# Moving x and u by 96 bytes inside their partitions in a transformer block kernel

## The chip, the cores and the metric

The kernel runs on one core of one Trainium2 chip. The metric is the time of one execution in microseconds (us) on the device; the kernel before was run three times. A profile is one further execution, recorded instruction by instruction. Engines are called as the profile calls them: PE is TensorE's matmul stream, PEld its weight loads, DVE is VectorE, ACT is ScalarE, POOL is GpSimd, SP is SyncE.

## The reference

One block over 256 tokens of width 1024, in float32: an RMS norm, one wide input projection, causal attention with 8 heads beside a gated depthwise convolution with a layer norm, an output projection with residual, a second RMS norm, a gated feed-forward network of width 2816 with residual, and a last RMS norm. Cut to what matters:

```python
u = rms_norm(h, mix_norm_g[l])
proj = u @ w_in[l]                                   # 1024 x 2560
q, k, v, glu_a, glu_g = jnp.split(proj, splits, axis=-1)
attn_out = moba_attention(heads(q), heads(k), heads(v), rel_bias)
conv_out = conformer_conv(glu_a, glu_g, conv_w[l], conv_b[l], conv_ln_g[l], conv_ln_b[l])
h = h + jnp.concatenate([attn_out, conv_out], axis=-1) @ w_out[l]
u = rms_norm(h, ffn_norm_g[l])
h = h + (jax.nn.silu(u @ w_gate[l]) * (u @ w_up[l])) @ w_down[l]
return rms_norm(h, final_norm_g)
```

With 256 tokens the attention has one block of keys, so only the causal part of it is left.

## The kernel before, in words

Every large product is made from float32 operands that are split in two: a rounded upper part and the remainder, so that a product takes three matmuls: upper by upper, upper by lower, lower by upper. For the weights, `high` makes the upper part `wh` (a copy on ACT, for two pieces on DVE) and `split` the lower part `wl` (a subtraction on DVE). For the activations, the upper part `uh` and the lower part `ul` lie in one tile, `u2`, of 8 row blocks by 2 parts by 256 tokens; `xs` holds x (later the hidden state) in 8 row blocks of 256 tokens. `xs` and `u2` come from the pool `const`, the first in memory, and the weights' parts `wh_...` and `wl_...` from the pool `wts` right behind it.

A matmul has two operands in SBUF: the stationary one, 128 columns that a weight load brings into the array ahead of it, and the moving one, which streams past. Each matmul here has a weight load of its own. Which operand is u differs from stage to stage, and so does the length of the stream:

- the input projection's convolution half (`a_mm`, outputs `pa` and `pg`) and its queries and keys (`qk_mm`, outputs `pqk`): weights stationary, u moving, 256 columns;
- the values (`v_mm`, output `pv`): u stationary, weights moving, 512 columns;
- the output projection (`o_part`, output `py`): weights stationary, moving the tiles `mh` and `ml` (the upper and lower part of the attention and convolution outputs), 256 columns;
- gate and up projection (`up_mm`, output `pf`): u stationary, weights moving, 512 columns; 48 matmuls for each of 11 groups of 256 hidden units;
- the down projection (`down`, output `pd`): stationary `fh` and `fl`, the two parts of the gated activations, weights moving, 512 columns, 24 matmuls for each group; its last quarters (output `pe`) have streams of 256 columns.

The order of the first part, up to the end of the output projection, is written out by hand in the string `PROGRAM`; after it, groups of `pf` and `pd` alternate, `down(g - 1)` behind `gate_up(g + 1)`. SP issues the loads of the weights in that order, two tensors ahead. PE, and every engine, keeps its instructions in program order.

Places in a partition, in bytes, of the built programs (the remainder by 128 in brackets). A tile's operands lie at its base plus multiples of 512 bytes, in the input, output, gate, up and down projections all.

| tile | before | after |
|---|---|---|
| `mhalf` (the exponent -0.5) | 42848 (96) | 16512 (0) |
| `xs` | 16512 (0) | 16608 (96) |
| `u2` | 24704 (0) | 24800 (96) |
| `pv` (vectors) | 41088 (0) | 41184 (96) |
| `ones`, `ident` | 41824, 42336 (96) | 41984, 42496 (0) |
| first `wh` buffer; all `wh`, `wl` and raw weights alike | 72800 (96) | 72928 (96) |
| first `fh` buffer; all `fh`, `fl` alike | 183392 (96) | 183520 (96) |
| `mh`, `ml` | 203520, 212736 (0) | 203648, 212864 (0) |

Of the kernel before, what the change touches and what calls it, by code (L numbers as in the profile page):

```python
# [10 lines left out]
F32 = mybir.dt.float32  # L11
F32R = mybir.dt.float32r
AF = mybir.ActivationFunctionType
ALU = mybir.AluOpType

P = 128
# [16 lines left out]
Q = 6  # L33
# [19 lines left out]
PV_G1, PV_G2, PV_CB, PV_LG, PV_LB, PV_T = 0, 8, 16, 20, 24, 28  # L53
PV_CW = PV_T + CC * ONV
PV_FOLD = PV_CW + 16 * Q
PV_N = PV_FOLD + 32
# [3 lines left out]
def block_kernel(ctx, tc, xT, w_in, w_out, w_gu, w_down, pvec, gfin, relb, hot, out):  # L60
    nc = tc.nc
    const = ctx.enter_context(tc.tile_pool(name="const", bufs=1))
# [8 lines left out]
    def mm(*args, **kw):  # L71
        return tc.keep_in_program_order(nc.tensor.matmul(*args, **kw))  # L72
# [12 lines left out]
    act, vec, pool, sync = (InOrder(e) for e in (nc.scalar, nc.vector, nc.gpsimd, nc.sync))  # L85

    def bank(i, name):
        return psum.tile([P, 512], F32, tag=f"b{i}", name=name)
# [76 lines left out]
        return mm(o, wl, uh, start=False, stop=stop, skip_group_check=True)  # L165


    xs = const.tile([P, KD, S], F32, name="xs")
    u2 = const.tile([P, KD, 2, S], F32R, name="u2")
    uh, ul = u2[:, :, 0], u2[:, :, 1]  # L170
    pv = const.tile([P, PV_N], F32, name="pv")
    ones = const.tile([P, P], F32, name="ones")
    ident = const.tile([P, P], F32, name="ident")
    mhalf = const.tile([P, 2], F32, name="mhalf")
    warm = const.tile([P, 1], F32, name="warm")
    accx = w1.tile([P, S], F32, name="accx")
    rbt = w1.tile([NB + 1, H], F32, name="rbt")
# [25 lines left out]
        pool.memset(t[:, TAPS - 1 + S : UW + TAPS - 1], 0.0)  # L203
        pool.memset(t[:, UW + TAPS - 1 + S :], 0.0)
    pool.memset(invc, 1.0 / (CC * P))
    pool.dma_start(pv[:, PV_T:], pvec[:, PV_T:])

    col = lambda lo, i: pv[:, lo + i : lo + i + 1]


    def conv_weights(half):
        fold, cw = pv[:, PV_FOLD:], pv[:, PV_CW + half * 8 * Q :]
        vec.tensor_tensor(
            wstk[half],
            bass.AP(tensor=fold.tensor, offset=fold.offset, ap=[fold.ap[0], [0, 8 * Q], [1, 32]]),
            bass.AP(tensor=cw.tensor, offset=cw.offset, ap=[cw.ap[0], [1, 8 * Q], [0, 32]]), op=ALU.mult)
# [3 lines left out]
    def rstd(acc, n, eps, name, b):  # L220
        ps = bank(b, f"ps_{name}")
        for t in range(2):
            mm(ps[:, t : t + 1], acc[:, t * P : (t + 1) * P], ones[:, 0:1], start=True, stop=True)
        ms = const.tile([P, 2], F32, name=f"ms_{name}")
        vec.tensor_scalar(ms, ps[:, 0:2], 1.0 / n, eps, op0=ALU.mult, op1=ALU.add)
        rc = const.tile([P, 2], F32, name=f"rc_{name}")
        pool.tensor_tensor(rc, ms, mhalf, op=ALU.pow)
        dg = const.tile([P, S], F32, name=f"dg_{name}", tag="dg")
        for t in range(2):
            vec.tensor_scalar(dg[:, t * P : (t + 1) * P], ident, rc[:, t : t + 1], None, op0=ALU.mult)  # L230
        return rc, dg
# [28 lines left out]
    cw = lambda c: csq[0][:, c]  # L260
# [74 lines left out]
    def scale_x():  # L335
        xn["c"], xn["d"] = rstd(accx, D, RMS_EPS, "x", 5)
# [147 lines left out]
    def norm(part):  # L484
        if part == 1:
            vec.tensor_add(s4[:, 0], s4[:, 0], s4[:, 1])
        elif part == 2:
            pm = bank(2, "pm")
            mm(pm[:, :S], invc, s4[:, 0], start=True, stop=True)
            for c in range(CC):  # L490
                vec.tensor_sub(cv(c), cv(c), pm[:, :S])
        elif part == 6:
            csq.append(w1.tile([P, CC, S], F32, name="csq", tag="wstk", bufs=2))
            for c in range(CC):
                act.activation(cw(c), cv(c), AF.Square)
        elif part == 3:
            vec.tensor_add(s4[:, 0], cw(0), cw(1))
            vec.tensor_add(s4[:, 1], cw(2), cw(3))
            vec.tensor_add(s4[:, 0], s4[:, 0], s4[:, 1])
        elif part == 7:  # L500
            _, ln["dg"] = rstd(s4[:, 0], CC * P, LN_EPS, "ln", 4)
        elif part == 4:
            ln["r"] = wide(ln["dg"], "ln", 5)
        else:
            for c in range(CC):
                vec.tensor_mul(cv(c), cv(c), ln["r"][:, :S])
                act.activation(cw(c), cv(c), AF.Silu, scale=col(PV_LG, c), bias=col(PV_LB, c))
                act.copy(mix[0][:, 4 + c], cw(c))
            for c in range(CC):
                vec.tensor_sub(mix[1][:, 4 + c], cw(c), mix[0][:, 4 + c].bitcast(F32))  # L510
# [13 lines left out]
    def a0(k):  # L524
# [7 lines left out]
           "a0": a0, "a1": a1, "glu": glu, "qk": qk_mm, "qo": qk_out, "sc": score, "t": logits, "n": normed, "fl": flip,  # L532
           "fo": flip_out, "v": v_mm, "pv": pv_mm, "mo": mix_out, "l": norm, "o": o_mm, "f": finish, "c": conv,
           "co": conv_out, "cw": conv_weights, "ct": conv_taps, "hs": lambda m: sumsq(acch, xs[:, m], m, "h"),
           "sq": lambda k: sumsq(accx, xs[:, k], k, "x"), "g": lambda m: lower_u(m, PV_G2)}
    for op, *args in steps:
# [95 lines left out]
    for k in range(KD):  # L632
        for t in range(2):
            up_mm(0, t, k)
        if k == 5:
            rc2, _ = rstd(acch, D, RMS_EPS, "h", next(spare))
            split("u1")
# [39 lines left out]
    for t in range(2):  # L677
# [27 lines left out]
        ms = w2.tile([P, 2], F32, name=f"fms{t}")  # L705
# [103 lines left out]
```

## Time and profile before

| | |
|---|---|
| runs | 300.75, 302.58, 302.85 us; median 302.58 |
| the profiled execution's own time | 301.12 us |
| its span, first to last instruction | 299.3 us |
| mean granted TensorE clock | 0.995 |
| PE busy | 97% of the span |
| DVE, ACT, POOL busy | 68%, 50%, 15% |
| DMA, mean rate | 213 GB/s |

The time of a run holds the span and some 1.8 us around it. A busy PE is not PE at its peak: the matmuls are pipelined, each row lasts longer than the distance to the next one, and what a stage costs is the distance from start to start.

### The profile page before, as it was taken

How to read it: one execution, taken by the hardware profiler on the slowest of the kernel's cores; microseconds unless marked ns; L12 is line 12 of the kernel's file. 1: busy time of each engine (PE TensorE's matmuls, PEld its weight loads, DVE VectorE, ACT ScalarE, POOL GpSimd, SP SyncE). 2: the span in 40 equal slices, each digit the busy share in tenths (PEclk: the TensorE clock that was granted, in tenths of full speed). 3: DMA queues.
4: the chain of work that ended last, by engine and by line, in shares of the span. 5: the costliest groups of instructions: out<-in, count | busy, mean ns of one | idle time of the engine just before them, and what ended most of it. 6: DMA issues, size and time to landing. Idle time of an engine off the chain costs nothing.

```text
span 299.3 us, 4767 instructions
## 1 busy us (share of the span) xinstructions
PE 291.7 (97%) x1750; PEld 246.0 (82%) x1750; DVE 203.5 (68%) x373; ACT 149.8 (50%) x255; POOL 44.2 (15%) x83
## 2 busy tenths in 40 slices
PE   8999999999999999999999999999999999999991
PEld 8999977897699988888888888888888888888880
DVE  3886999888987788957947548281838356321783
ACT  3894545274583678536817254361718163402542
POOL 4000100000000000143131313320431313130000
PEclk9999999999999999999999999999999999999998
DMA  6999879744418436888994949969794949420012
GB/s 189 369 409 333 247 190 297 285 141 143 128 21 293 146 117 171 283 315 275 343 324 116 314 125 308 307 209 365 234 285 143 302 112 313 149 70 1 0 64 78
DMA packets 21624, 63.73 MB, mean 213 GB/s; under 512 B 3117, under 2 KB 5957, under 8 KB 21600
## 3 DMA queue, kind: packets, MB, share of 16 engines
q1 hardware_dynamic: 18176, 54.99, 56.0%
q0 software_dynamic: 2992, 8.08, 9.6%
q10 hardware_dynamic: 432, 0.34, 0.3%
q8 instruction: 14, 0.23, 0.3%
q14 instruction: 10, 0.08, 0.1%
HBM read 58.08 MB, written 5.32 MB: 212 GB/s over the span
## 4 chain that ended last, share of the span: by engine, by line
PE 96%; issue 2%; DVE 0%; POOL 0%; POOLq 0%; ACT 0%; DVEq 0%; ACTq 0%
PE pf L72 41%; PE pd L72 18%; PE py L72 8%; PE pqk L72 8%; PE pa L72 4%; PE pv L72 4%; PE pg L72 4%; PE pc L72 4%; PE wm L72 1%; PE ps L72 1%; PE pt L75 1%; PE po L72 1%; PE pe L72 0%; PE pz L72 0%; POOLq L805 0%
## 5 line engine op out<-in xcount | busy, mean ns | idle before, releaser
L72 PE MATMUL pf<-wh_u,u 128*128 128x512 f32 x176 | 57.4, 396 | 0.0
L72 PE MATMUL pf<-wh_g,u 128*128 128x512 f32 x176 | 57.1, 395 | 0.0
L83 DVE TENSOR_TENSOR ff<-fs,pf 128x256 f32<-128x256 f32 x22 | 9.0, 418 | 56.8 <-ACT fs L83 56.8
L83 ACT ACTIVATE fs<-pf,rc_h 128x256 f32<-128x256 f32 x22 | 10.5, 476 | 69.8 <-PE pf L72 69.2
L72 PEld LDWEIGHTS pf<-wh_u,u 128*128 128x128 f32 x176 | 33.1, 188 | 7.9
L72 PEld LDWEIGHTS pf<-wh_g,u 128*128 128x128 f32 x176 | 33.1, 188 | 7.8
L72 PE MATMUL pf<-wl_u,u 128*128 128x512 f32 x88 | 34.8, 396 | 0.0
L72 PE MATMUL pf<-wl_g,u 128*128 128x512 f32 x88 | 34.8, 395 | 0.0
L72 PE MATMUL pd<-wh_d,fh 128*128 128x512 f32 x84 | 32.9, 392 | 0.0
L72 PE MATMUL pd<-wh_d,fl 128*128 128x512 f32 x84 | 32.8, 390 | 0.0
L72 PE MATMUL pd<-wl_d,fh 128*128 128x512 f32 x84 | 32.7, 389 | 0.0
L83 DVE TENSOR_TENSOR wl_u<-raw_u,wh_u 128x1024 fp32r<-128x1024 f32 x22 | 26.4, 1220 | 8.4 <-ACT wh_u L83 8.4
L83 POOL DMA_DIRECT2D fb<-fd x40 | 23.2, 586 | 47.7 <-DMA fd<-fv 13.9
L83 ACT CAST wh_u<-raw_u 128x1024 fp32r<-128x1024 f32 x22 | 22.7, 1051 | 14.3 <-PE pf L72 10.9
L83 DVE TENSOR_TENSOR wl_g<-raw_g,wh_g 128x1024 fp32r<-128x1024 f32 x22 | 25.9, 1216 | 1.5 <-ACT wh_g L83 1.5
L83 DVE TENSOR_TENSOR wl_d<-raw_d,wh_d 128x1024 fp32r<-128x1024 f32 x22 | 25.6, 1203 | 0.5 <-ACT wh_d L83 0.5
L72 PE MATMUL pqk<-u,wh_qk 128*128 128x256 f32 x128 | 23.1, 282 | 0.0
L83 ACT CAST wh_g<-raw_g 128x1024 fp32r<-128x1024 f32 x22 | 22.0, 1048 | 0.0
L83 ACT CAST wh_d<-raw_d 128x1024 fp32r<-128x1024 f32 x22 | 21.9, 1046 | 0.0
L72 PEld LDWEIGHTS pqk<-u,wh_qk 128*128 128x128 f32 x128 | 19.6, 188 | 0.4 <-issue 0.3
L72 PEld LDWEIGHTS pf<-wl_u,u 128*128 128x128 f32 x88 | 16.5, 188 | 4.0
L72 PEld LDWEIGHTS pf<-wl_g,u 128*128 128x128 f32 x88 | 16.5, 188 | 4.0
(154 smaller groups left out, 557.7 us busy)
## 6 DMA issues: line engine op xcount, KB each, us to landing
raw_g<-in_w_gu SPq DMA_DIRECT2D x22, 512.0 KB, 5.2
raw_u<-in_w_gu SPq DMA_DIRECT2D x22, 512.0 KB, 6.5
raw_d<-in_w_down SPq DMA_DIRECT2D x22, 512.0 KB, 4.7
raw_qk<-in_w_in SPq DMA_DIRECT2D x8, 512.0 KB, 7.3
raw_o<-in_w_out SPq DMA_DIRECT2D x8, 512.0 KB, 4.3
fd<-fv POOLq DMA_DIRECT2D x10, 256.0 KB, 4.1
fb<-fd POOLq DMA_DIRECT2D x40, 64.0 KB, 5.7
ustk<-ud SPq DMA_DIRECT2D x8, 288.0 KB, 5.6
```

The costliest lines, as they stand in the source:

```text
L72: return tc.keep_in_program_order(nc.tensor.matmul(*args, **kw))
L75: return tc.keep_in_program_order(nc.tensor.transpose(o, i, ident))
L83: return lambda *a, **k: tc.keep_in_program_order(f(*a, **k))
```

## The change

`mhalf`, two floats a partition, becomes a tile of 24 floats (96 bytes) and is allocated first instead of last among the constants, so that `xs` and `u2` start 96 bytes later. `pv` gets 16 floats (64 bytes) of padding; with it everything from `warm` on, the weights among it, starts 128 bytes later and so at the same place modulo 128. Readers of `mhalf` and `pv` name the columns that they read, since the tiles are now wider. The instructions, their shapes and their order on each engine are the same, but for the one memset of `mhalf`, which is 24 columns wide instead of 2.

```diff
+    mhalf = const.tile([P, 24], F32, name="mhalf")
     xs = const.tile([P, KD, S], F32, name="xs")
     u2 = const.tile([P, KD, 2, S], F32R, name="u2")
     uh, ul = u2[:, :, 0], u2[:, :, 1]
-    pv = const.tile([P, PV_N], F32, name="pv")
+    pv = const.tile([P, PV_N + 16], F32, name="pv")
     ones = const.tile([P, P], F32, name="ones")
     ident = const.tile([P, P], F32, name="ident")
-    mhalf = const.tile([P, 2], F32, name="mhalf")
     warm = const.tile([P, 1], F32, name="warm")
...
-    pool.dma_start(pv[:, PV_T:], pvec[:, PV_T:])
+    pool.dma_start(pv[:, PV_T:PV_N], pvec[:, PV_T:])
...
-        fold, cw = pv[:, PV_FOLD:], pv[:, PV_CW + half * 8 * Q :]
+        fold, cw = pv[:, PV_FOLD:PV_N], pv[:, PV_CW + half * 8 * Q :]
...
-        pool.tensor_tensor(rc, ms, mhalf, op=ALU.pow)
+        pool.tensor_tensor(rc, ms, mhalf[:, 0:2], op=ALU.pow)
```

## Rows read from the trace of the kernel before

**Rows 1.** The page: engines, and the chain that ended last.

```profile
PE 291.7 (97%) x1750; PEld 246.0 (82%) x1750; DVE 203.5 (68%) x373; ACT 149.8 (50%) x255; POOL 44.2 (15%) x83
...
PE 96%; issue 2%; DVE 0%; POOL 0%; POOLq 0%; ACT 0%; DVEq 0%; ACTq 0%
```

**Rows 2.** Waits of PE, whole span: total, times, longest.

```profile
PE wm L72 <- POOL ones L83: 1.0, 1, 1.0
```

**Rows 3.** Busy time by stretch, all engines: us (instructions); clock, DMA share, GB/s.

```profile
30.00:84.00 54.00, 54.00 (x517) 43.86 (x518) 50.06 (x125) 27.51 (x62) 1.17 (x2) 1.00 0.67 200
142.00:275.00 133.00, 133.00 (x577) 108.02 (x576) 71.06 (x101) 55.49 (x77) 29.16 (x46) 1.00 0.71 227
```

**Rows 4.** The chain from 108 us, in order: start, us, what.

```profile
108.44 8.39 PE pf L72 x36
...
117.16 25.32 PE pf L72 x108
...
225.72 5.45 PE pd L72 x24
231.17 11.20 PE pf L72 x48
242.37 5.45 PE pd L72 x24
...
278.61 2.77 PE pd L72 x12
```

**Rows 5.** Timeline of PE inside a block of pd: start, us.

```profile
244.70 0.39 PE L72 MATMUL pd<-wh_d,fl 128*128 128x512 f32 x1
...
246.51 0.39 PE L72 MATMUL pd<-wl_d,fh 128*128 128x512 f32 x1
```

**Rows 6.** The chain from 55 to 110 us.

```profile
62.48 2.81 PE pqk L72 x24
...
68.75 2.80 PE pv L72 x12
...
94.35 14.09 PE py L72 x120
```

**Rows 7.** The chain from 9 to 28 us, first and last of 30 steps.

```profile
9.37 0.24 PE pg L72 x2
...
23.37 0.24 PE pg L72 x2
```

**Rows 8.** Groups of PE by line and form: count, busy us, mean ns.

```profile
L72 PE MATMUL pqk<-u,wh_qk 128*128 128x256 f32 x128 | 23.1, 282 | 0.0
...
L72 PE MATMUL pqk<-u,wl_qk 128*128 128x256 f32 x64 | 17.9, 279 | 0.0
L72 PE MATMUL pa<-u,wh_a 128*128 128x256 f32 x64 | 13.6, 295 | 0.0
```

**Rows 9.** Timeline of PE in the first block of pe.

```profile
285.77 0.28 PE L72 MATMUL pe<-wh_d,fl 128*128 128x256 f32 x1
...
286.73 0.28 PE L72 MATMUL pe<-wl_d,fh 128*128 128x256 f32 x1
```

**Rows 10.** Weight loads of tile pe: ns min, median, max, first and last start.

```profile
L72 PEld LDWEIGHTS pe<-wh_d,fh x8: 188/192/192, 285.3 to 292.0; 128*128 128x128 f32 x8
```

**Rows 11.** Weight loads of tile pd.

```profile
L72 PEld LDWEIGHTS pd<-wh_d,fh x84: 187/188/192, 142.1 to 290.2; 128*128 128x128 f32 x84
```

**Rows 12.** Groups of DVE and ACT on tiles at remainder 96, and on xs.

```profile
L83 DVE TENSOR_TENSOR fl<-fb,fh 128x256 fp32r<-128x256 f32 x20 | 7.5, 419 | 2.3 <-ACT fh L83 2.3
L83 ACT CAST fh<-fb 128x256 fp32r<-128x256 f32 x20 | 7.1, 405 | 4.4 <-DMA fb<-fd 4.4
...
L83 DVE TENSOR_TENSOR xs<-py,xs 128x256 f32<-128x256 f32 x8 | 3.3, 420 | 0.8 <-PE py L72 0.7
...
L83 ACT ACTIVATE sq_x<-xs 128x256 f32<-128x256 f32 x7 | 2.5, 404 | 0.0
```

**Rows 13.** Tile ident, matmuls: ns min, median, max.

```profile
L75 PE MATMUL pt<-ident,p x24: 270/272/327, 48.7 to 81.1; 128*128 128x128 f32 x24
L75 PE MATMUL pt<-ident,ff x4: 270/272/275, 278.2 to 281.3; 128*128 128x128 f32 x4
```

## The prediction

> **What bounds the kernel now.** I read the page first: PE is busy 97% of the span, and the chain that ended last is PE for 96% of it [rows 1]. A chain that is nearly all one engine can still hold waits, so I looked at what PE waits for: one wait of 1.0 us, at the start, and none after [rows 2]. The granted clock is 1.00, the level of 2.4 GHz, in both long stretches [rows 3]. So from some 9 us to the last matmul the time is the sum of the distances from one matmul's start to the next, and anything that alters such a distance alters the time by as much. DVE is the only other engine that comes near its limit, 50.06 of 54.00 us between 30 and 84 us; in the long second part it is busy 71.06 of 133.00 us, ACT 55.49, and the DMA share is 0.71 [rows 3].
>
> The distances are therefore what to read. They come from the chain, where a piece of n matmuls has its whole length:
>
> - pf, 512 columns: 11.20 us for 48 [rows 4], 233.3 ns each.
> - pd, 512 columns: 5.45 us for 24 [rows 4], 227.1 ns; inside a block 1.81 us for 8 steps [rows 5], 226.3 ns. I take 226.7.
> - pv, 512 columns: 2.80 us for 12 [rows 6], 233.3 ns.
> - pqk, 256 columns: 2.81 us for 24 [rows 6], 117.1 ns; py, 256 columns: 14.09 us for 120 [rows 6], 117.4 ns; pa and pg, 256 columns: 14.00 us for 30 steps of four [rows 7], 116.7 ns.
> - pe, 256 columns: 0.96 us for 8 steps [rows 9], 120.0 ns.
>
> These stand out against what the streams alone need at 2.4 GHz, 213.3 and 106.7 ns. Two things do not fit a fixed cost for each matmul. First, pf and pd are the same operation in shape, in type, in the order of the three products, each with its weight load, and yet 6.6 ns apart. Second, pe is slower than pqk by 3 ns, although both stream 256 columns. The table of places gives both the same division: in pd and pe both operands lie at remainder 96 by 128; in pf, pv, pqk, pa and pg one is at 96 and u at 0; in py likewise, with `mh` and `ml` at 0. So operands at the same place take 226.7 and 120.0 ns, operands 32 bytes apart modulo 128 take 233.3 and 117. Above the bare streams that is 13.3 ns for either length at the same place, and 20 and 10 ns otherwise. In pe the weight loads themselves are longer, median 192 ns [rows 10] where pd's have 188 [rows 11]: with short streams the loads follow each other so closely that a delayed load delays the next. That reading is mine; the rows show the durations, not the cause.
>
> **The change part by part.** The instructions do not change. After it u lies at remainder 96 like the weights, so every product of u goes over to the case of pd and pe; pd, pe and py keep their relation, since all of their tiles move by 128.
>
> 1. pf: 36 and 108 matmuls and eight blocks of 48 (three of these ten pieces stand in [rows 4]; the other seven blocks repeat the one of 48), 528 in all. From 233.3 to 226.7 ns: 528 x 6.6 ns = 3.5 us gained. The bounds are the two rows themselves: nothing (233.3 stays) and 528 x 7.0 = 3.7 us (226.3, the inside of a block). I take the value of pd, whose operation is the same.
> 2. pv: 48 matmuls in blocks of 12. A block of 12 of pd that follows other work took 2.77 us [rows 4], 231 ns each, so a short block need not reach the pace. Bounds: 48 x 2.3 = 0.1 and 48 x 6.6 = 0.3 us gained; I take 0.2.
> 3. pqk: 128 and 64 matmuls [rows 8]. From 117.1 to pe's 120.0 ns: 192 x 2.9 = 0.56 us lost. pa and pg: two halves of 8 row blocks with 12 matmuls each, 192 (pa's upper part alone has its 64 in [rows 8]). From 116.7 to 120.0: 192 x 3.3 = 0.63 us lost. Together 1.2 us. The bounds are 117, the price now (nothing lost), and 120 (1.2 us); a gain below 117 has no row here. I take pe, the only stream of u's new relation with 256 columns.
> 4. Engines that read xs or write u: at remainder 96 ACT's 128x256 cast takes 405 ns, and its square of xs, at remainder 0, 404; DVE's 128x256 subtraction 419, its sum on xs 420 [rows 12]. No difference to multiply: nothing, either way within 1 ns on some 60 instructions, 0.1 us, which PE's stream hides from 9 us on.
> 5. `ident` goes to remainder 0. Its transposes are 24 from p, at 0, and 4 from ff, at 96; both have a median of 272 ns [rows 13] in opposite relations, so I book nothing. The wider memset of `mhalf` has its first reader, the power for the first norm, far behind the first matmuls.
>
> What hides a faster pf is the room on the other engines: 3% less time for the second part still leaves DVE at some 55%, ACT at 43% and the DMA at 0.73 of it. If that cover were gone, a block of pf would wait for the split of its weights and the 3.5 us would be given back. In the first part a slower pqk gives DVE, the fuller engine there, a little more time.
>
> Sum: 3.5 + 0.2 - 1.2 = 2.5 us less. Against the profiled execution, 301.12 us with span 299.3, that is 298.6. The median of the runs, 302.58, lies 1.5 us above that execution, with the same work; I take the difference off the median: **300.1 us**, 0.8% less.
>
> Against it speaks a rule of the Trainium skill (TensorE: Matmul & The Clock Gate, Part 2: What happens when you issue a matmul): PE has two independent SBUF read ports, so that loading the next weights does not take read bandwidth from the running matmul. By that rule places would not matter, which is the second rival below, and the sum would be 0; pf and pd, equal but for their places and 6.6 ns apart [rows 4], do not agree with it.
>
> **The rivals.**
>
> - *Short streams are not charged.* pe's 120 ns might belong to something else, such as standing right behind pd at the end; it is 24 matmuls in two blocks. Then the gain of pf and pv stands alone: 302.58 - 3.7 = 298.9 us. For it: only one place shows 120. Against it: the longer weight loads, 192 ns, in exactly that place [rows 10].
> - *Places do not matter.* pf and pd also differ in the bank order of their outputs (pf holds one bank for three matmuls and changes between two token halves; pd between four banks) and in how far apart the operands lie (u 48 KB or more below the weights, fh up to 110 KB above). If one of these makes the 6.6 ns, the time stays: 302.6 us. Against it: the pitch of pf is the same in all blocks although the buffers of its weights rotate.
> - *Slower: the short streams pay and the long ones gain nothing.* The place is pa, pg and pqk, in the first part; the price is the 1.2 us above, if u at the weights' remainder brings pe's 120 ns while pf's 233.3 has the cause of the rival before. That gives 303.8 us. It decides from where pf gains less than 1.2 us / 576 = 2.1 ns a matmul, that is stays above 231.2.
> - *The change does not do what it says:* the table of places in the built programs shows that xs and u2 do move by 96 and the weights by 128, so I give this nothing.
>
> **How the numbers follow.** The forecast has 0.54, the short streams uncharged 0.22, no effect 0.15, slower 0.09. 1% of 302.58 is 3.0 us, about what a measurement of this kernel can tell from no change. The first rival lies beyond it, and of the forecast about a quarter, since its 2.5 us reach it with the upper bound of pf and half the price of the short streams: 0.22 + 0.14 = 0.36 faster by over 1%. The slower rival lies within 1% by its own price, 1.2 us; with the spread of the runs, some 2 us, less than half of it passes: 0.04. The rest, 0.60, is within 1%. The range goes from the first rival less half of the spread of the runs, 297.8, to no effect with the highest run's distance above the median, 302.9; what is left out is the slower rival and the far ends.
>
> **What would show it.** In the chain after: a block of 48 pf at 10.88 us instead of 11.20, pd unchanged at 5.45 for 24, 24 pqk at 2.88 instead of 2.81, four pa and pg at 0.48 instead of 0.467, py at 117.4 still. Weight loads of pqk at 192 ns instead of 188 would bear out the short streams' price. The forecast is wrong if pf stays at 233, if pqk stays at 117 or falls, or if PE shows waits in front of pf.

## The result, and the profile after

The changed kernel takes 299.18 us (median of 6 runs, 298.61 to 299.85), the kernel before in the same measurements 301.94 us (6 runs, 300.75 to 302.85). The ratio is 0.9905, 95% interval 0.9879 to 0.9932: 2.8 us less. The forecast was 300.1 us, 0.8% less. The two profiled executions, 301.12 and 299.41 us, lie only 1.7 us apart, since that of before was among its fastest. Comparisons leave out single executions that ran far longer than the rest (364 to 589 us); the profiled execution of one experiment, e9_64_and_0, was such a one (417 us, granted clock 0.658), so it gives a time here and no rows.

The page of the changed kernel, busy time and the chain that ended last:

```profile
PE 289.9 (97%) x1750; PEld 247.4 (83%) x1750; DVE 203.7 (68%) x373; ACT 150.1 (50%) x255; POOL 44.3 (15%) x83
...
PE 88%; DMA 4%; issue 2%; ACT 2%; SPq 1%; DVE 1%; POOLq 0%; POOL 0%; DVEq 0%; ACTq 0%
```

PE is as busy as before, but 8% of the chain has left it [rows 1], all of it ahead of 24.4 us. The chain in order of time shows what the streams take now (start, us, what):

```profile
23.95 0.44 DVE accx L83
...
24.43 0.61 PE ps_x L72 x4
...
25.62 0.24 PE pa L72 x2
...
27.54 0.24 PE pa L72 x2
...
31.33 8.64 PE pqk L72 x72
...
63.95 2.88 PE pqk L72 x24
...
70.36 2.75 PE pv L72 x12
...
86.31 5.89 PE py L72 x48
...
95.91 14.24 PE py L72 x120
110.15 8.17 PE pf L72 x36
...
143.32 5.44 PE pd L72 x24
148.76 10.88 PE pf L72 x48
...
283.95 1.45 PE pe L72 x12
```

A block of 48 pf takes 10.88 us, 226.7 ns each, where it took 11.20 [rows 4]; all eight blocks read 10.88. pd stays at 5.44 for 24. A block of 24 pqk takes 2.88 us, 120.0 ns, where it took 2.81 [rows 6], and pv 2.75 for 12 instead of 2.80. Between the two rows of pa lie 16 matmuls of pa and pg in 1.92 us, 120.0 ns each, where the kernel before has 116.7 [rows 7]. py, whose price the sum left alone, takes 14.24 us for 120 instead of 14.09 [rows 6]. The weight loads of pqk (ns min, median, max) have changed too:

```profile
L72 PEld LDWEIGHTS pqk<-u,wh_qk x128: 186/192/192, 31.0 to 69.8; 128*128 128x128 f32 x128
```

Their median is 192 ns, as in pe [rows 10] and not as in pd [rows 11].

Where the time went is read from the starts of the stages. Three rows of the chain of the kernel before, which answer to the rows above:

```profile
30.12 8.45 PE pqk L72 x72
...
84.76 5.89 PE py L72 x48
...
285.70 1.45 PE pe L72 x12
```

| stage | before, us | after, us | difference | in the sum |
|---|---|---|---|---|
| start to pqk | 30.12 | 31.33 | +1.21 | +0.63 |
| pqk to py (pqk, pv) | 54.64 | 54.98 | +0.34 | +0.36 |
| py to pf | 23.68 | 23.84 | +0.16 | 0 |
| pf to pe | 177.26 | 173.80 | -3.46 | -3.5 |
| pe to the end | 13.60 | 13.55 | -0.05 | 0 |

The sum of the differences, -1.80 us, is that of the spans, 299.3 and 297.5. Two stages, pqk to py and pf to pe, came out as forecast. py to pf lost 0.16 us that the sum put at nothing. The first one lost twice its term in this execution; one part of it is a wait that is new, in the list of the weight loads (PEld):

```profile
PEld ps_x L72 <- DVE accx L83: 0.3, 1, 0.3
```

The matmul that sums x's squares over the partitions, `ps_x`, waits here for DVE's running sum `accx`, whose last step ends at 24.39 us in the chain above; before, no weight load had such a wait. There the sum was done at 22.73 us and `ps_x` began at 23.45, by the timeline of before:

```profile
21.25 1.48 DVE L83 TENSOR_TENSOR accx<-accx,sq_x 128x256 f32<-128x256 f32 x3
23.45 0.50 PE L72 MATMUL ps_x<-ones,accx 128*128 128x1 f32 x4
```

### The profile page after: what moved, and what is told of

It is laid out like the page before. It is cut to its first block, busy times and chain, and to the rows that moved or that the text cites. A ratio compares the mean times of both kernels' runs of the same rounds, so it can differ in the third digit from the quotient of the medians.

```text
span 297.5 us, 4767 instructions
## 1 busy us (share of the span) xinstructions
PE 289.9 (97%) x1750; PEld 247.4 (83%) x1750; DVE 203.7 (68%) x373; ACT 150.1 (50%) x255; POOL 44.3 (15%) x83
## 4 chain that ended last, share of the span: by engine, by line
PE 88%; DMA 4%; issue 2%; ACT 2%; SPq 1%; DVE 1%; POOLq 0%; POOL 0%; DVEq 0%; ACTq 0%
PE pf L72 40%; PE pd L72 18%; PE pqk L72 8%; PE py L72 8%; DMA raw_a<-in_w_in 4%; PE pv L72 4%; PE pc L72 4%; SPq L83 1%; PE ps L72 1%; PE pt L75 1%; PE pa L72 1%; ACT wh_a L83 1%; PE pg L72 1%; PE po L72 1%; ACT sq_x L83 1%
## 5 line engine op out<-in xcount | busy, mean ns | idle before, releaser
L72 PE MATMUL pf<-wh_u,u 128*128 128x512 f32 x176 | 56.2, 390 | 0.0
L72 PE MATMUL pf<-wh_g,u 128*128 128x512 f32 x176 | 56.0, 389 | 0.0
L72 PE MATMUL pf<-wl_u,u 128*128 128x512 f32 x88 | 34.2, 389 | 0.0
L72 PE MATMUL pf<-wl_g,u 128*128 128x512 f32 x88 | 34.2, 389 | 0.0
```

## The experiments

All kernels but the last start from the kernel before. Of the edits the lines that matter are shown, some of them cut short. Distances are those of u from the weights modulo 128 bytes: +32 before, 0 after. Where u is moved alone, `u2` is a tile with 32 floats more, read at an offset; all tiles behind it move by 128 bytes.

**u alone, x and the rest unmoved** (e1_u_only)

```diff
-    u2 = const.tile([P, KD, 2, S], F32R, name="u2")
+    u2 = const.tile([P, KD * 2 * S + 32], F32R, name="u2")
+    u2 = u2[:, 24 : 24 + KD * 2 * S].rearrange("p (k t s) -> p k t s", k=KD, t=2)
```

> u alone moves to remainder 96 by 128, x, ident and ones keep their remainders. Theory (what counts is the place of u against the weights): a block of 48 pf takes 10.88 us, 24 pqk 2.88 us, py stays near 14.1 to 14.2 us for 120, and the time is that of the changed kernel, ratio to the kernel before 0.988 to 0.993. Rival (the move of x, or of ident, has a part in it): the time differs from the changed kernel's by more than 0.3%, in the stages before 31 us or in the transposes.

Measured: 299.09 us, ratio 0.9889 (0.9859 to 0.9919). Its chain:

```profile
64.11 2.88 PE pqk L72 x24
...
96.09 14.09 PE py L72 x120
...
148.75 10.88 PE pf L72 x48
```

The paces of u's products are those of the changed kernel and so is the time. The move of x, `ident`, `ones` and `pv` has no part in the time that can be seen; the one pace that differs is py's, 14.09 us for 120 as in the kernel before, against 14.24.

**Weights moved to u's old remainder** (e2_both_at_0)

```diff
-    acch = const.tile([P, S], F32, name="acch")
+    acch = const.tile([P, S + 8], F32, name="acch")[:, 0:S]
```

> u stays at remainder 0 and everything from the weights on moves by 32 bytes, so that weights, fh and fl lie at remainder 0 too; mh and ml keep 32 bytes to the weights. Theory (the relative place counts): pf 10.88 us for 48, pqk 2.88 for 24, pd 5.44 for 24, ratio 0.988 to 0.993, as the changed kernel. Rival (remainder 96 itself is good for long streams and bad for short ones): pf stays at 11.20, pqk at 2.81, pd rises from 5.45 towards 5.6, ratio 1.00 to 1.005.

Measured: 298.90 us, ratio 0.9881 (0.9846 to 0.9917).

```profile
63.19 2.88 PE pqk L72 x24
...
142.56 5.44 PE pd L72 x24
148.00 10.88 PE pf L72 x48
```

With u and the weights at remainder 0 the paces are the same as with both at 96. The rival of the absolute remainder falls: what counts is the place of one operand against the other. The first stage of this execution, as that of before, has no wait for `accx`, and pqk starts 0.44 us later than before, for the 0.63 of the sum:

```profile
30.56 8.64 PE pqk L72 x72
```

**Each norm's u at its own place** (e3_by_stage): u of the first norm at distance 32, u of the second at 0, by two views of the wider tile.

```diff
+    u2v = [u2[:, o : o + KD * 2 * S].rearrange("p (k t s) -> p k t s", k=KD, t=2) for o in (0, 24)]
...
-        mm(pf[g][t], uh[:, k, tok], wh, start=k == 0, stop=False)
+        mm(pf[g][t], uh2[:, k, tok], wh, start=k == 0, stop=False)
```

> u of the first norm stays at remainder 0, u of the second norm is written at remainder 96. Theory: pa, pg and pqk keep 117 ns (24 pqk 2.81 us), pv keeps 233 ns, pf takes 10.88 us for 48; 3.5 us less than before, 298.4 us, ratio 0.986 to 0.990, about 0.9 us below the changed kernel. Rival (the short streams were not charged by the place but by what else the change did): pqk is at 120 ns here too, and the time is the changed kernel's, ratio 0.9905.

Measured: 298.64 us, ratio 0.9876 (0.9843 to 0.9908).

```profile
31.86 8.54 PE pqk L72 x72
...
51.41 2.82 PE pqk L72 x24
54.89 2.85 PE pqk L72 x24
...
148.98 10.88 PE pf L72 x48
```

pf has its 10.88 us, and pqk is back below 2.88, but mostly at 2.85 for 24 where the kernel before has 2.81 to 2.83. So distance 32 modulo 128 does not fix the price of a short stream. One thing differs from the kernel before: the wider tile puts the weights 128 bytes farther from u, and no run tells whether that is the cause. The gain over u alone beside it, some 0.5 us by the medians, is half of what was expected, and the intervals overlap. pqk starts at 31.86 us here, later than in the changed kernel, although pa and pg have their old distance; there is a wait for `accx` in this execution too:

```profile
PEld ps_x L72 <- DVE accx L83: 0.7, 1, 0.7
```

**Other distances** (e4_other_places, e5_places_2, e6_places_3): the edit of the run before, with other pairs of offsets.

```diff
-  for o in (0, 24)]
+  for o in (16, 8)]      # e4: distance -32 for the first norm, 64 for the second
+  for o in (8, 28)]      # e5: 64 and 16
+  for o in (28, 16)]     # e6: 16 and -32
```

> u of the first norm at remainder 64, 32 bytes below the weights instead of 32 above, u of the second norm at remainder 32, 64 bytes from the weights. Theory in its narrow form (only the same place is special): pqk 117 ns and pv 233 as before, pf 233 ns, 11.20 us for 48. Rival (the distance counts in steps): pqk differs from 117 and 120, or pf from 233 and 227, by over 2 ns.

> u of the first norm at remainder 32, 64 bytes from the weights; u of the second norm at remainder 112, 16 bytes above the weights. Distance theory (the price of a place depends on its distance to the weights modulo 128; so far 0: 227 ns, 32: 233, 64: 229 for long streams): pv near 229 ns, pf between 227 and 233. Rival (only multiples of 32 matter): pf at 226.7 exactly, as at distance 0.

> u of the first norm 16 bytes above the weights, u of the second norm at remainder 64, 32 bytes below the weights. Distance theory: pf near 233 ns if only the size of the distance counts, as at 32 above; pqk between 117 and 120. Rival (the direction counts): pf differs from 233 by over 2 ns.

One execution each: 298.96, 298.23 and 302.38 us. The chain of e4, second norm at distance 64:

```profile
147.58 10.99 PE pf L72 x48
```

That is 229.0 ns, neither 233.3 nor 226.7: the narrow theory, in which only the same place is special, falls. The chain of e6, second norm 32 below:

```profile
149.31 11.19 PE pf L72 x48
```

233.1 ns, as 32 above: for pf the size of the distance counts, not its direction. Short streams are not so uniform: e6's first norm, at distance 16, has

```profile
54.41 2.80 PE pqk L72 x24
...
67.36 2.85 PE pqk L72 x24
```

The chain of e5, first norm at 64, second at 16:

```profile
52.98 2.74 PE pqk L72 x24
55.72 2.75 PE pv L72 x12
...
65.76 2.83 PE pqk L72 x24
68.59 2.80 PE pv L72 x12
...
116.97 25.30 PE pf L72 x108
...
147.72 10.88 PE pf L72 x48
```

Here one place has two paces. The first 108 pf run at 234.3 ns, about as the same 108 do at distance 32, 25.32 us [rows 4], and from the first block of pd on, which PE leaves at its own 226.7 ns, all eight blocks of pf hold 226.7 as well. That is the figure of the rival, by which only multiples of 32 matter, but the first 108 do not fit it; the distance theory put pf between 227 and 233. Neither holds. The instructions and the operands' distance are the same in both parts of pf; what ran before them differs, and so does what the other engines do meanwhile. That the work ahead of a block picks its pace is therefore a reading, not shown. At distance 64 pqk has two paces as well, 2.74 us for one block and 2.83 for others, and so has pv, 2.75 and 2.80. pa and pg take a faster pace for a stretch there, on e5's timeline of PE:

```profile
28.29 0.39 PE L72 MATMUL pa<-u,wl_a 128*128 128x256 f32 x2
...
29.88 0.39 PE L72 MATMUL pg<-u,wl_a 128*128 128x256 f32 x2
```

7 steps of two in 1.59 us are 113.6 ns, where the kernel before had 116.7 [rows 7] and the changed one has 120.

**Other lengths** (e7_lengths at distance 0, e8_lengths_apart at 32): every stream of pf cut in two, each part with its weight load.

```diff
+        for c in (slice(0, 384), slice(384, 512)):
+            mm(o, uh[:, k, tok], wh[:, c], start=st, stop=False, skip_group_check=True)
...
```

> u at the weights' remainder, and each pf stream of 512 columns cut into 384 and 128, with a weight load for each. If the price at the same place is 13.3 ns for each weight load: 173.3 ns a stream of 384, and 128 columns bound by the weight load at some 120 ns. If it is a share of the stream (6.25%): 170 ns. The time rises by about 528 x 66 ns = 35 us against the changed kernel.

> The same cut with u 32 bytes apart from the weights, as before the change. If the price there is a share of the stream (9.4%): 175 ns for 384 columns; if it is 20 ns for each: 180 ns. 128 columns are bound by the weight load, 107 to 120 ns.

331.98 and 330.64 us. A block of 96 in the chain of e7:

```profile
157.50 13.76 PE pf L72 x96
```

and in that of e8:

```profile
156.75 13.71 PE pf L72 x96
```

860 and 857 ns for three streams of 384 and three of 128. At distance 0 the two formulas give 880 and 870 with 120 ns for the short streams, and neither is borne out; at 32 they reach from 846 to 900, too wide to tell them apart. So the runs do not tell a price per weight load from a share of the stream. What they do show is that distance 0 has no advantage in this mix. e8 has one thing more. Its first norm lies as in e3, 32 from the weights, and its first 72 pqk take

```profile
30.91 8.63 PE pqk L72 x72
```

119.9 ns each, as at distance 0, where e3 has 8.54 us and the kernel before 8.45. Up to there e3 and e8 have the same instructions with their operands at the same places, and yet run at two paces.

**The best places put together** (e9_64_and_0: first norm at 64, second at 0; e10_and_py: `mh` and `ml` at 64 from the weights as well).

```diff
-  for o in (0, 24)]
+  for o in (8, 24)]
...
-            mix.extend(w1.tile([P, KD, S], F32R, name=n, tag="stk", bufs=2) for n in ("mh", "ml"))
+            for n in ("mh", "ml"):
+                t = w1.tile([P, KD * S + 8], F32R, name=n, tag="stk", bufs=2)
+                mix.append(t[:, 8 : 8 + KD * S].rearrange("p (k s) -> p k s", k=KD))
```

> u of the first norm 64 bytes from the weights, u of the second norm at their remainder. If the places add up stage by stage: pa and pg 113.3 ns, pqk 113 or 118 by block, pv near 229, pf 226.7; against the kernel before 0.65 us less in pa and pg, 0.3 less up to py, 3.5 less in pf: 4.4 us less, ratio 0.985; 1.6 us below the changed kernel. Rival (what a place gives in a short stream is lost in the waits of the first stages): the time of the changed kernel, ratio 0.9905.

> As the one before, and mh and ml at 64 bytes from the weights instead of 32. If py takes the pace of pa there, 113.3 ns: 120 py in 13.6 us instead of 14.1, and 192 matmuls give 0.8 us; if it takes the other pace of pqk, 118 ns: nothing. Ratio 0.982 or 0.985.

e9: 298.78 us, ratio 0.9890 (0.9868 to 0.9911). e10: 297.80 us, ratio 0.9864 (0.9831 to 0.9896). e9 does not reach the 0.985 of its places; the rival's 0.9905, the time of the changed kernel, lies in its interval. e10's interval holds the 0.985 that was expected if py takes the slower pace, and leaves out the 0.982. The chain of e10:

```profile
86.25 5.64 PE py L72 x48
...
95.50 14.13 PE py L72 x120
...
148.25 10.88 PE pf L72 x48
```

py gains 0.25 us in its first 48 and nothing in the last 120, which took the slower pace. In the first stage there is a wait:

```profile
PEld ps_x L72 <- DVE accx L83: 0.9, 1, 0.9
```

The weight load of `ps_x` stands 0.9 us for the sum of squares, which DVE makes behind the splits of the weights. In such an execution a faster pace of pa and pg gains nothing up to there. But the faster pace does not make the wait: e3, with pa and pg at their old distance, stood 0.7 us. The sum was done at 24.5 us here and at 25.0 in e3, against 22.7 in the kernel before; why so late is not shown. e10 is the fastest kernel by its median, 1.3 us below the changed kernel beside it, but their intervals overlap.

**The changed kernel again** (e11_changed_again)

> The changed kernel once more, beside these on the same chip: ratio 0.988 to 0.993 if its first measurement holds; pf 10.88 us for 48 and pqk 2.88 for 24 as in the first profile. The stage of pa and pg, 1.2 us longer in the first profile than before, comes back nearer to the 0.6 us of the sum if its rest was that execution's own.

Measured: 299.06 us, ratio 0.9900 (0.9879 to 0.9920).

```profile
30.87 8.64 PE pqk L72 x72
...
148.29 10.88 PE pf L72 x48
```

pqk starts at 30.87 us, 0.75 us later than before instead of 1.21: the first stage's excess over the forecast was for the larger part that execution's own. In e1, with the same paces, it starts at 31.48, in e2 at 30.56, and at distance 32 at 30.12 in the kernel before, 30.91 in e8 and 31.86 in e3. One execution's start of pqk thus does not give the price of a place.

## Why the prediction was right

1. *What bounds the kernel.* PE's starts did set the time from the first pqk on. Before that the reading was too simple. PE's own list of waits, which the prediction read, shows nothing after the start in either kernel; a matmul's wait for its operand stands in the list of the weight loads. There before had no wait for `accx`, since the sum was done 0.7 us ahead of `ps_x`, and that cover went in some executions. The mechanism was there to see in the order of the program.
2. *pf*, 3.5 us gained: measured 3.46 in the stage. The pace of pd, taken over as it stood, was exact, and four more kernels with pf at distance 0 repeat it (e1, e2, e3, e10).
3. *pv*, 0.2 us: 2.75 instead of 2.80 us for 12 is 0.05 us a block in three of the four, 0.17 us in all.
4. *pqk, pa and pg*, 1.2 us lost: pqk's 2.88 us for 24, 0.48 for four pa and pg and the weight loads' 192 ns are as forecast. pqk and pv together gave +0.34 us for +0.36. The first stage gave +1.21 and +0.75 us in two executions of the changed kernel and +0.44 in e2 for +0.63, but also +1.74 in e3, where pa and pg kept their distance, so the 0.63 is borne out by the pace alone. And at distance 32 the price is no constant: 8.45, 8.54 and 8.63 us for the same 72 pqk.
5. *Engines and transposes*, nothing: u moved alone gives the time of the whole change, 299.09 and 299.18 us, so no price of x's new place is seen. py should have kept its 117.4 ns and did not: 14.24 us for 120 are 118.7 ns, 0.15 us lost that the sum has not.
6. *The rivals.* Short streams uncharged: refuted by pqk's 2.88. No effect: refuted, the same instructions with u 96 bytes further take 10.88 instead of 11.20 us. By the Trainium skill's rule of two independent SBUF read ports (TensorE: Matmul & The Clock Gate, Part 2: What happens when you issue a matmul), as the prediction reads it, nothing should have changed; the measured 0.32 us less for a block decides against that reading. Slower: its condition, pf above 231.2 ns, did not come about.
7. *The whole.* That 2.8 us by the medians come so near the forecast's 2.5 is in part luck: the two profiled executions differ by 1.8 us of span, pqk starts anywhere from 30.1 to 31.9 us, and the forecast stood on a median of 302.58 us where six runs give 301.94. What the traces bear out is the stretch from pqk to the end, 3.0 us less, where the sum has 3.1.

Where the explanation was too narrow is that two cases, same place or 32 bytes apart, were taken for all there is. The runs show at least three paces for long streams (226.7, 229.0, 233.3 ns) and more than one pace at the same place. That did not touch the forecast, since at distance 0 each length was seen at one pace only, 226.7 and 120.0 ns; it fits with the version by stage gaining less than the sum says, though that shortfall is not clear of noise. Why the place of the operands has this effect is not shown by any run here. Nor is the unit of 128 bytes tested for pf: wherever operands shared a remainder they were a whole multiple of 512 bytes apart (u and the weights 48128, `fh` and the weights 110592), and no run has pf at 128 or 256 bytes more.

## What to carry to other kernels

Where every matmul has its own weight load, compare starts of equal matmuls across stages: a few nanoseconds between two groups of the same shape are a finding, and the places of their operands modulo 128 bytes are a thing to check. In these runs the streams of 512 columns were nowhere faster than with stationary and moving operand at the same place, while those of 256 gained nothing there (120.0 ns, elsewhere 113.6 to 119.9). One tile that serves both lengths may thus be worth laying out for each use apart; here that gave some 0.5 us, not clear of noise. Read the waits of the weight loads too, not those of the matmuls alone. And before a gain of a fraction of a microsecond is booked on a stage without waits, look how much later its next operand could have come.

## What the runs showed of the hardware that was not expected

By distance modulo 128 bytes between stationary and moving operand, from the chains, ns for one matmul:

| distance | 512 columns | 256 columns |
|---|---|---|
| 0 | 226.7 | 120.0 |
| 16 | 226.7 or 234.3 | 116.7 to 118.8 |
| 32, above or below | 233.3, 233.1 | 116.7 to 119.9 |
| 64 | 229.0; one block of 12 pv 233.3 | 113.6 to 118 |

At one and the same place a stream can hold either of two paces for a hundred matmuls; what picks it, no run separates. And py, whose operands kept their distance in all kernels up to e9, took 14.08 or 14.09 us for 120 in the kernel before, e1 and e3 to e8, and 14.24 in e2 and in both executions of the changed kernel; that this is the same effect is not shown.
